# In sparse-attention branch B the parts of v become the stationary operand and the transposed probabilities of all tokens the moving one

## The chip, the cores and the metric

The program runs on one core of one Trainium2 chip. The metric is device microseconds for one execution of the whole program, which covers both layers; lower is better. The core has a matrix engine (TensorE, "PE" in the profile, with its weight loads listed apart as "PEld"), a vector engine (VectorE, "DVE"), a scalar engine (ScalarE, "ACT"), GpSimd ("POOL") and a sync engine that issues the DMAs ("SP").

## The reference

Two layers of a decoder trunk for 512 tokens of width 1024. Each layer projects the normed tokens, runs three token mixers A, B and C, multiplies each projected branch by a sigmoid gate, sums, projects out, and then runs a gated feed-forward network with a short convolution. Branch B is what the change touches: a small indexer has picked, for each query, its best causal keys, and four heads of 64 attend over these.

```python
def mixer_sparse(q, k, v, q_idx, k_idx, w_idx):
    ...
        att = jnp.einsum('bqhd,bqkhd->bhqk', qb, k_sel).astype(jnp.float32) * (HEAD_DIM ** -0.5)
        valid = idx <= qpos[None, :, None]
        att = jnp.where(valid[:, None], att, -jnp.inf)
        p = jax.nn.softmax(att, axis=-1).astype(v.dtype)
        return jnp.einsum('bhqk,bqkhd->bqhd', p, v_sel)
...
    y = (gates[:, :, 0] * (o_a @ w_br_a) + gates[:, :, 1] * (o_b @ w_br_b)
         + gates[:, :, 2] * (o_c @ w_br_c))
    return y @ w_out
```

In the kernel nothing is gathered: keys that were not picked get -1e30 from a mask, so a head's probabilities for a tile of 128 queries are a 128 x (128 (t+1)) block row, t = 0 to 3.

## The kernel before

**Numbers in two parts.** Matmul operands are in the type fp32r. To keep accuracy each operand is split into a high and a low part: `split` has ACT copy the high part (L81) and DVE subtract it from the source (L82). An ordinary product is then three matmuls (`mm3`, L88 to L90: high by high, high by low, low by high). A matmul here has a stationary operand of 128 x 128, loaded by an instruction of its own, and a moving operand of up to 512 columns.

**The order of the work.** `ORDER` lists, per layer, the projections of A, the indexer, C, B ("B", 0 and "B", 1, two heads each) and between and after them the gated branch projections ga, gc, gb. The last entries are B 0, B 1, gc (8 column blocks) and gb (8 column blocks). Attention is cut into chains of three steps S, T and V. `slot()`, called once after every projection tile and every column block of a branch, issues the T of one chain, the S of the next and the V of the one before, so that attention is woven into projections; functions given to `later` run some slots on. Before gb begins, slots are called until all chains are done (gb needs B's outputs `oTb`). The tile framework then orders each engine's instructions from a simulated timeline, so the order in the trace is not the program's to the letter: matmuls of a later block can be put among those of a chain.

**A chain of B** (`chains_b`). For a unit of two heads there are six chains: three groups of query tiles (`PARTS`: tiles 0 and 1; tile 2; tile 3) by two heads.
- S: score matmuls (L396, L397) into a PSUM bank `sc`; `masked_exp` adds the mask and takes the maximum on DVE (L470) and the exponential on ACT with the row's sum (L472), into `e`.
- T: `transpose_p` transposes the 128 x 128 blocks of `e` on PE (L477) into a bank `tp`, and splits it in one piece into `ph` and `pl` (L480, which are L81 and L82 on tiles `pt`). Per head there are 3 + 3 + 4 = 10 blocks.
- V: `pv_mm`, per block: the block of `ph` is stationary and v's high and low parts move (128 columns, L488), then the block of `pl` is stationary and v's high part moves (64 columns, L489). Outputs come with queries on partitions.

After two query tiles of both heads `PV.evac` adds the two column halves on DVE (L525). At the end DVE takes the reciprocal of the row sums (L648), multiplies the outputs by it (L650), and `to_oT` transposes four blocks on PE (L532) and splits them (L81, L82 on tiles `u`) into `oTb[i]`, which gb's matmuls (L88 to L90, `mm<-u`) read.

Branch C has chains of the same form, with two score rows each and a DVE step on their ratio (L675 to L680) before its transposes.

Of the kernel before, what the change touches and what calls it, by code (L numbers as in the profile page):

```python
# [9 lines left out]
F32 = mybir.dt.float32  # L10
F32R = mybir.dt.float32r
# [3 lines left out]
ALU = mybir.AluOpType  # L15
AX = mybir.AxisListType

P = 128
LO, HI = HALF = slice(0, 64), slice(64, 128)
S = 512  # L20
NT = S // P
# [3 lines left out]
HD = 64  # L25
# [24 lines left out]
def tile_trunk(ctx, tc, x, positions, w_in, w_br_a, w_br_b, w_br_c, w_out, lam_q1, lam_k1, lam_q2, lam_k2,  # L50
               subln_g, norm_mix_pre, norm_mix_post, norm_ffn_pre, norm_ffn_post,
               w_ffn_up, conv_w, conv_b, w_ffn_down, out):
    nc = tc.nc
# [7 lines left out]
    def alloc(shape, dtype, tag):  # L61
        uid[0] += 1
        return sb.tile(shape, dtype, tag=tag, name=f"{tag}{uid[0]}", bufs=SBUF_SLOTS[tag])

    def palloc(tag):
        uid[0] += 1
        return ps.tile([P, 512], F32, tag=tag, name=f"{tag}{uid[0]}",
                       bufs=PSUM_BANKS[tag])

    def small(n=8):  # L70
        return alloc([P, n], F32, "s")
# [7 lines left out]
    def split(hi, lo, src, scale=None):  # L79
        if scale is None:  # L80
            nc.scalar.copy(hi, src)  # L81
            nc.vector.tensor_tensor(lo, src, hi.bitcast(F32), op=ALU.subtract)  # L82
        else:
            nc.scalar.activation(hi, src, AF.Copy, scale=scale)
            nc.vector.scalar_tensor_tensor(lo, src, scale, hi.bitcast(F32), op0=ALU.mult, op1=ALU.subtract)
# [61 lines left out]
    for g in range(3):  # L147
        for p in range(2):
            b = 768 * g + p * P
            unit_cols["A", g, p] = [(b, P), (b + 256, P), (b + 512, P)]  # L150
    unit_cols["A", 0, 0] = unit_cols["A", 0, 0] + [(OFF_I + 512, 72)]
    for h in range(4):
        b = OFF_C + h * P
        unit_cols["C", h] = [(b, P), (b + 512, P), (b + 1024, P)]
    for p in range(2):
        b = OFF_B + p * P
# [57 lines left out]
    ident = cp.tile([P, P], F32, name="ident")  # L214
# [104 lines left out]
    chains = []  # L319
# [5 lines left out]
    def later(f, lag=1):  # L325
        pending.append([lag, f])
# [138 lines left out]
    def qk_mm(dst, qkT, h, q0, k0, n):  # L465
        ks = slice(k0, k0 + n)
        score_mm(dst, qkT[:, h, q0:q0 + P], qkT[:, 2 + 2 * h, ks], qkT[:, 3 + 2 * h, ks])

    def masked_exp(e, sc, mask, mneg, dcol):
        nc.vector.tensor_tensor_reduce(out=e, in0=sc, in1=mask, scale=-0.125, scalar=3e38,  # L470
                                       op0=ALU.add, op1=ALU.min, accum_out=mneg)
        nc.scalar.activation(e, e, AF.Exp, bias=mneg, scale=-1.0, accum_out=dcol)  # L472

    def transpose_p(e, nb):
        tp = palloc("tp")
        for b in range(nb):
            nc.tensor.transpose(tp[:, b * P:(b + 1) * P], e[:, b * P:(b + 1) * P], ident)  # L477
        ph = alloc([P, 512], F32R, "pt")
        pl = alloc([P, 512], F32R, "pt")
        split(ph[:, 0:nb * P], pl[:, 0:nb * P], tp[:, 0:nb * P])  # L480
        return ph, pl

    def pv_mm(dst, pT, blocks):

        nb = len(blocks)
        for i, (b, v) in enumerate(blocks):
            c = slice(b * P, (b + 1) * P)
            nc.tensor.matmul(dst, pT[0][:, c], v, start=i == 0, stop=False)  # L488
            nc.tensor.matmul(dst[:, 0, :], pT[1][:, c], v[:, 0, :], start=False, stop=i == nb - 1)  # L489


    PARTS = [[(0, 0), (1, P)], [(2, 0)], [(3, 0)]]

    class Chain:


        def __init__(self, S_, V_, fin=None):
            self.S_, self.V_, self.fin = S_, V_, fin

        def S(self):  # L500
            self.e, self.nb = self.S_()

        def T(self):
            self.pT = transpose_p(self.e, self.nb)

        def V(self):
            self.V_(self.pT)
# [20 lines left out]
    def to_oT(o, oTs, i, scale=None, lag=1):  # L528
        def go():
            tp = palloc("tp")  # L530
            for t in range(NT):
                nc.tensor.transpose(tp[:, t * P:(t + 1) * P], o[:, t, :], ident)  # L532
            oT = alloc([P, 2, S], F32R, "u")
            split(oT[:, 0, :], oT[:, 1, :], tp, scale=scale)
            oTs[i] = oT
        later(go, lag)
# [82 lines left out]
    def chains_b(qkT, v, masks, oTs, i):  # L619
        while score_jobs:  # L620
            score_jobs.pop(0)()
        while topk_steps:
            if next(topk_steps[0], None) is None:
                topk_steps.pop(0)
        pv = PV(2)
        dd = alloc([P, NT, 2], F32, "s")
        on = alloc([P, NT, P], F32, "th")
        for parts in PARTS:
            for h in range(2):
                def S_(parts=parts, h=h):  # L630
                    sc = palloc("sc")
                    e = alloc([P, 512], F32, "sm")
                    for t, c0 in parts:
                        qk_mm(sc[:, c0:c0 + (t + 1) * P], qkT, h, t * P, 0, (t + 1) * P)
                    for t, c0 in parts:
                        sl = slice(c0, c0 + (t + 1) * P)
                        mneg = small()
                        masked_exp(e[:, sl], sc[:, sl], masks[t], mneg[:, 0:1], dd[:, t, h:h + 1])
                    return e, sum(t + 1 for t, _ in parts)

                def V_(pT, parts=parts, h=h):
                    for t, c0 in parts:
                        pv_mm(pv.at(t, h), pT, [(c0 // P + b, v[:, b, h]) for b in range(t + 1)])
                        if t % 2 == 1 and h == 1:
                            pv.evac(t // 2, on[:, t - 1:t + 1, :])

                def fin():
                    nc.vector.reciprocal(dd, dd)  # L648
                    onv = on.rearrange("p t (h d) -> p t h d", h=2)
                    nc.vector.tensor_tensor(onv, onv, dd.unsqueeze(3).to_broadcast([P, NT, 2, HD]), op=ALU.mult)  # L650
                    to_oT(on, oTs, i)
                chains.append(Chain(S_, V_, fin if (parts, h) == (PARTS[-1], 1) else None))


    def chains_c(qkT, v, nlam, subg, oTs, i):
# [159 lines left out]
    for l in range(DEPTH):  # L815
# [21 lines left out]
        masks = [cmask[:, 384:512], wkB, wkA[:, 512:896], wkA[:, 0:512]]  # L837
# [3 lines left out]
        for u in ORDER:  # L841
# [20 lines left out]
            elif u[0] == "A":  # L862
                g, p = u[1], u[2]
# [7 lines left out]
                else:  # L871
                    def go(p=p, vq=vq):
                        def fin(opn):
                            on = combine_a(a1[p, 0]["o0"], a1[p, 0]["md"], opn)
                            to_oT(on, oTa, p, lag=4)
                        chains_a12(*a1[p, 1][::-1], *vq[::-1], a_scr[l][p], fin)
# [42 lines left out]
        for t in range(NT):  # L919
            acc = palloc(("sc", "mm", "mm", "mm")[t])  # L920
# [119 lines left out]
```

## Time and profile before

| | us |
|---|---|
| median of 3 runs | 1857.63 |
| lowest, highest | 1857.12, 1858.28 |
| the profiled execution, its own time | 1860.71 |
| its span from first to last instruction | 1858.9 |

The profile is of one execution. Busy times are per engine. A matmul's length in the trace is from its start to a modelled end, and neighbours overlap in it; the distance from one matmul's start to the next one's is what a matmul costs the engine. Starts are in us from the start of the span. A group's row has its instructions' count, busy us and mean ns, then the idle time of the engine just before them and what ended it.

### The profile page before, as it was taken

How to read it: one execution, taken by the hardware profiler on the slowest of the kernel's cores; microseconds unless marked ns; L12 is line 12 of the kernel's file. 1: busy time of each engine (PE TensorE's matmuls, PEld its weight loads, DVE VectorE, ACT ScalarE, POOL GpSimd, SP SyncE). 2: the span in 40 equal slices, each digit the busy share in tenths (PEclk: the TensorE clock that was granted, in tenths of full speed). 3: DMA queues.
4: the chain of work that ended last, by engine and by line, in shares of the span. 5: the costliest groups of instructions: out<-in, count | busy, mean ns of one | idle time of the engine just before them, and what ended most of it. 6: DMA issues, size and time to landing. Idle time of an engine off the chain costs nothing.

```text
span 1858.9 us, 25416 instructions
## 1 busy us (share of the span) xinstructions
PE 1834.1 (99%) x9565; PEld 1607.4 (86%) x9565; DVE 1155.1 (62%) x2138; ACT 867.7 (47%) x1518; POOL 28.3 (2%) x53
## 2 busy tenths in 40 slices
PE   8999999999999999999999999999999999999998
PEld 6999989988889888888889999789888798888886
DVE  6687798665457666642367787885545566666332
ACT  5665654463335444432256756545533354444221
POOL 0000000000000000000000000000000000000000
PEclk9999999999999999999999999999999999999999
DMA  5333323233343333333433333232332443332241
GB/s 162 90 80 101 85 66 84 70 91 90 104 143 121 105 102 91 96 100 126 127 105 84 80 99 89 78 79 77 97 98 86 149 123 98 103 94 91 102 152 64
DMA packets 265173, 185.22 MB, mean 100 GB/s; under 512 B 14710, under 2 KB 238298, under 8 KB 265050
## 3 DMA queue, kind: packets, MB, share of 16 engines
q1 hardware_dynamic: 265050, 183.60, 33.8%
q8 instruction: 75, 1.23, 0.3%
q14 instruction: 48, 0.39, 0.1%
HBM read 171.99 MB, written 11.57 MB: 99 GB/s over the span
## 4 chain that ended last, share of the span: by engine, by line
PE 67%; issue 20%; DVE 7%; DMA 3%; ACT 2%; SPq 1%; POOL 0%; DVEq 0%; POOLq 0%; ACTq 0%
PE mm L88 16%; PE mm L89 16%; PE mm L90 16%; PE sc L88 2%; PE sc L89 2%; PE sc L90 2%; PE pv L488 2%; PE sc L396 1%; PE sc L397 1%; PE tp L477 1%; DMA wr<-in_w_in_dram 1%; DVE wl L82 1%; PE pv L89 1%; PE pv L88 1%; PE pv L90 1%
## 5 line engine op out<-in xcount | busy, mean ns | idle before, releaser
L82 DVE TENSOR_TENSOR wl<-wr,wh 128x1024 fp32r<-128x1024 f32 (+2 forms) x314 | 359.1, 1146 | 369.5 <-ACT wh L81 368.6
L81 ACT CAST wh<-wr 128x1024 fp32r<-128x1024 f32 (+2 forms) x314 | 309.4, 989 | 458.0 <-PE mm L90 135.5
L88 PE MATMUL mm<-xh,wh 128*128 128x512 f32 (+1 forms) x784 | 297.6, 380 | 1.3 <-ACT xh L81 0.8
L89 PE MATMUL mm<-xl,wh 128*128 128x512 f32 (+1 forms) x784 | 297.3, 379 | 0.0
L90 PE MATMUL mm<-xh,wl 128*128 128x512 f32 (+1 forms) x784 | 297.2, 379 | 0.0
L89 PE MATMUL mm<-wl,xh 128*128 128x384 f32 (+2 forms) x816 | 283.0, 348 | 0.9 <-DVE wl L82 0.9
L90 PE MATMUL mm<-wh,xl 128*128 128x384 f32 (+2 forms) x816 | 283.6, 348 | 0.0
L88 PE MATMUL mm<-wh,xh 128*128 128x384 f32 (+2 forms) x816 | 281.5, 348 | 1.3 <-ACT xh L81 0.7
L88 PEld LDWEIGHTS mm<-xh,wh 128*128 128x128 f32 x784 | 147.9, 189 | 27.8 <-ACT xh L81 1.2
L89 PEld LDWEIGHTS mm<-xl,wh 128*128 128x128 f32 x784 | 147.7, 188 | 26.2 <-DVE xl L82 0.4
L90 PEld LDWEIGHTS mm<-xh,wl 128*128 128x128 f32 x784 | 147.8, 188 | 26.1
L89 PEld LDWEIGHTS mm<-wl,xh 128*128 128x128 f32 x816 | 154.4, 189 | 5.7 <-DVE wl L82 1.9
L88 PEld LDWEIGHTS mm<-wh,xh 128*128 128x128 f32 x816 | 154.4, 189 | 5.7 <-ACT xh L81 1.7
L90 PEld LDWEIGHTS mm<-wh,xl 128*128 128x128 f32 x816 | 154.4, 189 | 4.0 <-DVE s L226 0.3
L90 PE MATMUL sc<-xh,wl 128*128 128x512 f32 (+1 forms) x272 | 99.2, 365 | 0.0
L89 PE MATMUL sc<-xl,wh 128*128 128x512 f32 (+1 forms) x272 | 99.0, 364 | 0.0
L88 PE MATMUL sc<-xh,wh 128*128 128x512 f32 (+1 forms) x272 | 98.8, 364 | 0.0
L88 PE MATMUL mm<-wh,qk 128*128 128x512 f32 x216 | 85.8, 397 | 0.0
L89 PE MATMUL mm<-wl,qk 128*128 128x512 f32 x216 | 85.4, 396 | 0.0
L90 PE MATMUL mm<-wh,qk 128*128 128x512 f32 x216 | 85.1, 396 | 0.0
L488 PE MATMUL pv<-v,pt 128*128 128x128 f32 (+1 forms) x280 | 71.2, 297 | 2.7 <-ACT pt L81 2.7
L472 ACT ACTIVATE sm<-sm,s 128x128 f32<-128x128 f32 (+2 forms) x96 | 53.5, 558 | 43.3 <-DVE s L470 43.1
(274 smaller groups left out, 3251.8 us busy)
## 6 DMA issues: line engine op xcount, KB each, us to landing
wr<-in_w_ffn_up_dram SPq DMA_DIRECT2D x176, 256.0 KB, 3.4
wr<-in_w_in_dram SPq DMA_DIRECT2D x282, 128.0 KB, 2.5
wr<-in_w_in_dram SPq DMA_DIRECT2D x56, 512.0 KB, 3.9
wr<-in_w_ffn_down_dram SPq DMA_DIRECT2D x44, 512.0 KB, 3.7
wr<-in_w_out_dram SPq DMA_DIRECT2D x16, 512.0 KB, 3.6
xd<-u SPq DMA_DIRECT2D x12, 512.0 KB, 3.7
u<-xd SPq DMA_DIRECT2D x12, 512.0 KB, 5.2
u<-in_x_dram SPq DMA_DIRECT2D x8, 512.0 KB, 5.9
```

Source lines behind the costliest of these rows:

```text
L81: nc.scalar.copy(hi, src)
L82: nc.vector.tensor_tensor(lo, src, hi.bitcast(F32), op=ALU.subtract)
L88: nc.tensor.matmul(dst, a[0], b[0], start=start, stop=False)
L89: nc.tensor.matmul(dst, a[0], b[1], start=False, stop=False)
L90: nc.tensor.matmul(dst, a[1], b[0], start=False, stop=stop)
L396: nc.tensor.matmul(dst, q, kh, start=True, stop=False)
L397: nc.tensor.matmul(dst, q, kl, start=False, stop=True)
L472: nc.scalar.activation(e, e, AF.Exp, bias=mneg, scale=-1.0, accum_out=dcol)
L477: nc.tensor.transpose(tp[:, b * P:(b + 1) * P], e[:, b * P:(b + 1) * P], ident)
L488: nc.tensor.matmul(dst, pT[0][:, c], v, start=i == 0, stop=False)
```

## The change

In `chains_b` the operands of the last product change places. v's high and low parts side by side (128 columns of one key block and head) are stationary, and the transposed probabilities move, for all query tiles that can see this key block at once: 512, 384, 256 and 128 columns for key blocks 0 to 3. High and low parts of the probabilities are moved one after the other, so a head has 8 matmuls into one bank `acc`. Its rows 0 to 63 are the part from v's high half and rows 64 to 127 that from v's low half; ACT copies the lower one out and DVE adds them. The output then has its dimension on partitions and tokens along the columns, as `oTb` needs it.

For this the transposed blocks of all of a head's chains are kept in one tile `g` (a buffer of the kind `qk`), and are split into it by query tile, and tile 3's fourth block apart: five splits for a head where there were three. The matmuls of a head all stand in V of its last chain. Chains run head by head instead of group by group. As queries are now columns, the rows' sums can't be applied at the end, so each S takes their reciprocal and scales `e`. The end of a unit is a split of `of` without transposes.

```diff
--- before.py
+++ after.py
@@ -494,14 +494,14 @@
     class Chain:
 
 
-        def __init__(self, S_, V_, fin=None):
-            self.S_, self.V_, self.fin = S_, V_, fin
+        def __init__(self, S_, V_, fin=None, T_=None):
+            self.S_, self.V_, self.fin, self.T_ = S_, V_, fin, T_ or transpose_p
 
         def S(self):
             self.e, self.nb = self.S_()
 
         def T(self):
-            self.pT = transpose_p(self.e, self.nb)
+            self.pT = self.T_(self.e, self.nb)
 
         def V(self):
             self.V_(self.pT)
@@ -622,11 +622,11 @@
         while topk_steps:
             if next(topk_steps[0], None) is None:
                 topk_steps.pop(0)
-        pv = PV(2)
-        dd = alloc([P, NT, 2], F32, "s")
-        on = alloc([P, NT, P], F32, "th")
-        for parts in PARTS:
-            for h in range(2):
+        dd = alloc([P, 2, NT, 2], F32, "md")
+        of = alloc([P, S], F32, "th")
+        for h in range(2):
+            hold = []
+            for parts in PARTS:
                 def S_(parts=parts, h=h):
                     sc = palloc("sc")
                     e = alloc([P, 512], F32, "sm")
@@ -635,21 +635,51 @@
                     for t, c0 in parts:
                         sl = slice(c0, c0 + (t + 1) * P)
                         mneg = small()
-                        masked_exp(e[:, sl], sc[:, sl], masks[t], mneg[:, 0:1], dd[:, t, h:h + 1])
+                        masked_exp(e[:, sl], sc[:, sl], masks[t], mneg[:, 0:1], dd[:, 0, t, h:h + 1])
+                    t0, t1 = parts[0][0], parts[-1][0] + 1
+                    nc.vector.reciprocal(dd[:, 1, t0:t1, h], dd[:, 0, t0:t1, h])
+                    for t, c0 in parts:
+                        sl = slice(c0, c0 + (t + 1) * P)
+                        nc.vector.tensor_scalar(e[:, sl], e[:, sl], dd[:, 1, t, h:h + 1], None, op0=ALU.mult)
                     return e, sum(t + 1 for t, _ in parts)
 
-                def V_(pT, parts=parts, h=h):
+                def T_(e, nb, parts=parts, hold=hold):
+
+
+                    if not hold:
+                        hold.append(alloc([P, 6, S], F32R, "qk"))
+                    g = hold[0]
+                    tp = palloc("tp")
+                    for b in range(nb):
+                        nc.tensor.transpose(tp[:, b * P:(b + 1) * P], e[:, b * P:(b + 1) * P], ident)
                     for t, c0 in parts:
-                        pv_mm(pv.at(t, h), pT, [(c0 // P + b, v[:, b, h]) for b in range(t + 1)])
-                        if t % 2 == 1 and h == 1:
-                            pv.evac(t // 2, on[:, t - 1:t + 1, :])
+                        n = min(t + 1, 3)
+                        ts = slice(t * P, (t + 1) * P)
+                        split(g[:, 0:n, ts], g[:, 3:3 + n, ts], tp[:, c0:c0 + n * P].rearrange("p (b c) -> p b c", b=n))
+                        if t == 3:
+                            split(g[:, 1, 0:P], g[:, 4, 0:P], tp[:, 384:512])
+                    return g
+
+                def V_(g, parts=parts, h=h):
+                    if parts is not PARTS[-1]:
+                        return
+                    acc = palloc("pv")
+                    for b in range(NT):
+                        row, cols = (b, slice(b * P, S)) if b < 3 else (1, slice(0, P))
+                        for w in range(2):
+                            nc.tensor.matmul(acc[:, b * P:S], v[:, b, h].rearrange("p s d -> p (s d)"),
+                                             g[:, 3 * w + row, cols], start=b + w == 0, stop=b == 3 and w == 1)
+                    low = alloc([P, S], F32, "pt")
+                    nc.scalar.copy(low[LO], acc[HI])
+                    nc.vector.tensor_tensor(of[HALF[h]], acc[LO], low[LO], op=ALU.add)
 
                 def fin():
-                    nc.vector.reciprocal(dd, dd)
-                    onv = on.rearrange("p t (h d) -> p t h d", h=2)
-                    nc.vector.tensor_tensor(onv, onv, dd.unsqueeze(3).to_broadcast([P, NT, 2, HD]), op=ALU.mult)
-                    to_oT(on, oTs, i)
-                chains.append(Chain(S_, V_, fin if (parts, h) == (PARTS[-1], 1) else None))
+                    def go():
+                        oT = alloc([P, 2, S], F32R, "u")
+                        split(oT[:, 0, :], oT[:, 1, :], of)
+                        oTs[i] = oT
+                    later(go)
+                chains.append(Chain(S_, V_, fin if (parts, h) == (PARTS[-1], 1) else None, T_))
 
 
     def chains_c(qkT, v, nlam, subg, oTs, i):
```

## Rows read from the trace of the kernel before

**Rows 1.** The page's parts on the whole span: busy time of the engines, and the clock granted to PE in 40 slices of the span (9 is 90% or more of full speed).
```profile
PE 1834.1 (99%) x9565; PEld 1607.4 (86%) x9565; DVE 1155.1 (62%) x2138; ACT 867.7 (47%) x1518; POOL 28.3 (2%) x53
...
PEclk9999999999999999999999999999999999999999
```

**Rows 2.** The chain of work that ended last, by engine, as shares of the span ("issue" is time in which nothing that the profile shows was waited for).
```profile
PE 67%; issue 20%; DVE 7%; DMA 3%; ACT 2%; SPq 1%; POOL 0%; DVEq 0%; POOLq 0%; ACTq 0%
```

**Rows 3.** Busy time by stretch, one stretch among B's chains in each layer: length, then busy us (and instructions) of PE, PEld, DVE, ACT and POOL, PE's granted clock, share of the DMA engines, GB/s.
```profile
435.00:455.00 20.00, 20.00 (x102) 16.94 (x101) 8.75 (x14) 6.51 (x11) 0.00 (x0) 1.00 0.30 79
...
1360.00:1380.00 20.00, 20.00 (x103) 16.94 (x102) 9.79 (x17) 7.46 (x14) 0.00 (x0) 1.00 0.30 82
```

**Rows 4.** Groups on PE from 383 to 478 us, the stretch of layer 0 in which B's chains run: the two matmuls of a block, and the transposes of the outputs.
```profile
L488 PE MATMUL pv<-v,pt 128*128 128x128 f32 x40 | 9.5, 283 | 0.0
L489 PE MATMUL pv<-v,pt 128*128 128x64 f32 x40 | 9.0, 240 | 0.0
...
L532 PE MATMUL tp<-ident,th 128*128 128x128 f32 x8 | 1.2, 272 | 0.0
```

**Rows 5.** PE in order of time, the first and the last of eight matmuls of one chain of B that stand together, L489 and L488 by turns, and the two 512-column matmuls behind them (start, length, engine, line).
```profile
1391.21 0.19 PE L489 MATMUL pv<-v,pt 128*128 128x64 f32 x1
...
1391.91 0.31 PE L488 MATMUL pv<-v,pt 128*128 128x128 f32 x1
1392.06 0.45 PE L88 MATMUL mm<-xh,wh 128*128 128x512 f32 x1
1392.34 0.40 PE L89 MATMUL mm<-xl,wh 128*128 128x512 f32 x1
```

**Rows 6.** PE in order of time, unbroken streams of one width: the first and the last of eight matmuls of 512 columns, of four of 384, of four of 256. Then, from the page's groups, the matmuls of one line of `mm3` and the weight loads of that line.
```profile
300.77 0.34 PE L90 MATMUL mm<-wh,xl 128*128 128x384 f32 x1
...
301.29 0.34 PE L90 MATMUL mm<-wh,xl 128*128 128x384 f32 x1
...
568.03 0.28 PE L90 MATMUL mm<-xh,wl 128*128 128x256 f32 x1
...
568.38 0.28 PE L90 MATMUL mm<-xh,wl 128*128 128x256 f32 x1
...
1400.09 0.39 PE L88 MATMUL mm<-xh,wh 128*128 128x512 f32 x1
...
1401.68 0.39 PE L89 MATMUL mm<-xl,wh 128*128 128x512 f32 x1
...
L89 PE MATMUL mm<-wl,xh 128*128 128x384 f32 (+2 forms) x816 | 283.0, 348 | 0.9 <-DVE wl L82 0.9
...
L89 PEld LDWEIGHTS mm<-wl,xh 128*128 128x128 f32 x816 | 154.4, 189 | 5.7 <-DVE wl L82 1.9
```

**Rows 7.** PE in order of time at the four output transposes of unit 0 of layer 0, merged into one row, and what follows.
```profile
438.86 0.60 PE L532 MATMUL tp<-ident,th 128*128 128x128 f32 x4
439.29 0.49 PE L477 MATMUL tp<-ident,sm 128*128 128x128 f32 x3
```

**Rows 8.** Groups on DVE and on ACT from 383 to 478 us that answer to operations which the change removes or adds, and one row in order of time, a tensor-by-constant operation on DVE.
```profile
L82 DVE TENSOR_TENSOR pt<-tp,pt 128x384 fp32r<-128x384 f32 x8 | 4.4, 553 | 0.5 <-ACT pt L81 0.5
L82 DVE TENSOR_TENSOR pt<-tp,pt 128x512 fp32r<-128x512 f32 x4 | 2.8, 689 | 2.9 <-ACT pt L81 2.9
L525 DVE TENSOR_REDUCE th<-pv 128x256 f32<-128x512 f32 x4 | 2.8, 688 | 4.5 <-PE pv L489 4.4
...
L650 DVE TENSOR_TENSOR th<-th,s 128x512 f32<-128x512 f32 x2 | 1.4, 692 | 0.1
L391 DVE TENSOR_TENSOR qk<-tp,qk 64x512 fp32r<-64x512 f32 x2 | 1.4, 684 | 0.6 <-ACT qk L390 0.6
...
L81 ACT CAST pt<-tp 128x384 fp32r<-128x384 f32 x8 | 3.8, 476 | 6.0 <-PE tp L477 6.0
...
L390 ACT CAST qk<-tp 64x512 fp32r<-64x512 f32 x4 | 2.3, 582 | 0.4 <-PE tp L425 0.4
...
344.25 0.42 DVE L748 TENSOR_SCALAR u<-u 128x512 f32<-128x512 f32 x1
```

**Rows 9.** All engines in order of time at the end of B in layer 1, from the last chain's transposes to the first matmul that reads unit 1's outputs (an idle time just before an instruction, and what ended it, stands in brackets).
```profile
1387.19 0.60 PE L477 MATMUL tp<-ident,sm 128*128 128x128 f32 x4
...
1393.66 0.24 PE L489 MATMUL pv<-v,pt 128*128 128x64 f32 x1
...
1397.24 0.50 PE L88 MATMUL mm<-xh,wh 128*128 128x512 f32 x1 [0.27 <-ACT th L762]
...
1397.87 0.68 DVE L82 TENSOR_TENSOR u<-tp,u 128x512 fp32r<-128x512 f32 x1
...
1401.90 0.61 PE L88 MATMUL mm<-u,wh 128*128 128x512 f32 x2
```

**Rows 10.** Busy time by stretch (columns as in rows 3) where slots run without a projection beside them, in branch C just ahead of ga, in layer 0 and in layer 1.
```profile
261.00:265.00 4.00, 2.16 (x14) 1.37 (x12) 4.00 (x10) 2.67 (x7) 0.00 (x0) 1.00 0.33 73
265.00:269.00 4.00, 3.66 (x16) 3.21 (x15) 4.00 (x11) 1.83 (x4) 0.00 (x0) 0.57 0.10 26
...
1177.00:1184.00 7.00, 4.05 (x20) 2.53 (x18) 7.00 (x19) 4.07 (x9) 0.80 (x1) 0.94 0.21 53
1184.00:1191.00 7.00, 7.00 (x25) 5.96 (x25) 6.92 (x16) 3.16 (x7) 0.00 (x0) 0.57 0.02 6
```

**Rows 11.** DVE in order of time in an S of branch C: the reciprocal of a row sum, and what it waited for.
```profile
342.14 0.17 DVE L675 RECIPROCAL s<-s 128x2 f32<-128x2 f32 x1 [0.99 <-ACT sm L472]
```

## Prediction, made before the change was run

> **What bounds the kernel now.** I read the page's sum of busy times first: PE is busy for 1834.1 of 1858.9 us, DVE for 62% and ACT for 47%, and the clock was at full speed in every slice [rows 1]. The reader should distrust the 99%, since neighbouring matmuls overlap in the records; so the chain of waits comes second: PE holds 67% of it, and most of the rest is "issue", in which nothing was waited for, while DMA has 3% and DVE 7% [rows 2]. The busy times by stretch among B's chains come third, because a mean over the span says nothing about the stage that changes. In both layers PE is busy there for 20.00 of 20 us, at a clock of 1.00, while DVE works 8.75 to 9.79 us, ACT 6.51 to 7.46, and the DMA engines 0.30 of the time [rows 3]. So in this stage PE sets the pace, and every microsecond that one of its instructions costs is a microsecond of the kernel. The last question is what an instruction costs on PE, and that is read from the distances between starts, not from lengths.
>
> **PE, the product with v.** In the stretch of layer 0 there are 40 blocks, each with a matmul of 128 columns and one of 64 [rows 4]: four heads with ten blocks, 20 matmuls a head, 8 heads in two layers. Eight of them stand together from 1391.21 to the 512-column matmul at 1392.06, whose own successor is at 1392.34 [rows 5]. An unbroken stream of 512 columns steps by (1401.68 - 1400.09) / 7 = 0.227 us [rows 6]. I take one such step off the 1.13 us: 0.90 us for eight, 0.113 us each, although four of them move 128 columns and four 64. At the 512-column pace of 0.44 ns a column those would be 0.057 and 0.028 us. The columns do not set this price; what each instruction has in common is a load of 128 x 128 of its own, as every matmul here has (816 matmuls and 816 loads of one line, rows 6). A head costs 20 x 0.113 = 2.26 us.
>
> After the change a head has two matmuls each of 512, 384, 256 and 128 columns. Streams give 0.227 us, 0.52 / 3 = 0.173 us and 0.35 / 3 = 0.117 us for the first three [rows 6]: the loads are inside these steps. For 128 columns I take 0.113. Sum: 2 x (0.227 + 0.173 + 0.117 + 0.113) = 1.26 us. A head saves 1.00 us, eight heads 8.0 us. Bounds: if no load were hidden, each of the eight would cost 0.113 us more and a head would save 0.10, all of them 0.8 us; if a 128-column matmul cost its columns alone, 0.057, a head would save 1.11 us, all of them 8.9. I take 8.0, as the streams in rows 6 are of the same form.
>
> **PE, the output transposes.** Eight in layer 0's stretch [rows 4], 16 in the kernel. Four take 439.29 - 438.86 = 0.43 us [rows 7], so 16 cost 1.7 us, all gone. The ten transposes of probabilities and the scores of each head stay. PE's sum: -8.0 - 1.7 = -9.7 us.
>
> A rule speaks against the first term. The Trainium skill, "TensorE: Matmul & The Clock Gate", section "Back-to-back issue gap", gives an isolated step of columns / 2.4 + 2.5 ns; an estimate by it is 0.85 us a head before and 1.09 us after, so 1.9 us lost over eight heads, and 0.9 us won on the transposes. Its section "LDWEIGHTS (loading the stationary operand)" gives columns / 1.2, an estimate of 0.107 us for 128, and the trace agrees with that one: 0.113 us whatever the columns.
>
> **DVE and ACT.** Per head DVE gets three reciprocals at 0.17 [rows 11], the scaling of 128 + 256 + 384 + 512 columns (0.42 us for 512 in the nearest row, a tensor by a constant, so 1.05 by columns; at the other end 0.69 for 512 as for the two-tensor operations, 1.7), and a final add of 64 x 512 at 0.684 [rows 8]. Its splits go from 2 x 0.553 + 0.689 to 2 x 0.553 and one of 256 and two of 128 columns; on the line through 0.553 and 0.689 those are 0.42 and 0.28, so 0.29 us more. It loses the evacuation (0.688 a head) and its share of the multiply (0.692 a unit, 0.35 a head). Net +1.5 to +2.2 us a head, 6 to 9 us per layer. ACT gets the copy of 64 x 512 at 0.582 and some 0.3 us of extra splits: +0.9 us a head, under 4 us per layer. The work that hides it is the projection and gate matmuls that PE does for some 95 us per layer: DVE has over 10 us idle in each 20, ACT over 12 [rows 3]. Priced at nothing; if that cover were gone it would be at most 9 + 4 us per layer.
>
> **Waits.** Each S now has DVE wait for ACT's row sum before its reciprocal; in branch C, which does this already, DVE sat 0.99 us [rows 11]. Behind it on DVE stand the low parts of the weights and the splits of other chains, and PE waits for the weights. There are 24 such S. PE showed no idle time among B's chains, and DVE's idle half covers it: nothing.
>
> All eight matmuls of a head now wait for the last split of its last chain, where earlier ones could start before. That matters once per layer, at the end of B, where gb needs unit 1's outputs. Before, the last transposes start at 1387.19, the last product ends at about 1393.7, the outputs are split by 1397.87 + 0.68 = 1398.55, and the first matmul that reads them starts at 1401.90 [rows 9]: 3.35 us of slack, filled with gate matmuls of the next block. After, S is longer by about 1.0 + 0.17 + 0.42 us, T by a small split, while behind the product come a copy of 0.58, an add of 0.68, and a split of about 0.58 + 0.69: 2.5 us where it was 4.8. The two balance, the slack stays, and I price it at nothing. No DMA is added, removed or moved. The four extra `qk` buffers per layer come round to ones whose readers are finished.
>
> **The sum.** 1860.7 us for the profiled execution (span 1858.9 and 1.8 around it) - 9.7 = 1851.0. The median is 3.1 us below that execution, so 1857.6 - 9.7 = 1847.9; I say 1848. A measurement of this kernel can tell about 0.2%, 3.7 us, from no change.
>
> **The rivals.**
> - Columns set the pace (the rule above, as a mechanism of this kernel). At 0.444 ns a column, a head goes from 1920 columns, 0.85 us, to 2560, 1.14: +2.3 us in all, and 16 transposes of 0.057 give back 0.9: +1.4, 1859 us. Rows 5 speak against it: 64 and 128 columns would not cost the same. 3%.
> - PE stalls at the end of B. Where slots run without cover, ahead of ga, PE did 2.16 of 4 us and then ran at a mean clock of 0.57, so partly at 1.2 of 2.4 GHz, for 4 us: 1.8 + 0.3 + 1.7 = 3.9 us lost; in layer 1 it was 2.95 + 0.4 + 3.0 = 6.4 us [rows 10]. Once per layer that takes back 3.9 to 12.8 us: between 1852 and 1861. It decides if the outputs come more than 3.35 us later than now [rows 9]. 10%.
> - DVE's waits reach PE, the case on the slower side. With none of 24 waits of 0.99 us covered, +23.8 - 9.7 = +14.1: 1872 us. The place is the S step; it ends slower once more than (9.7 + 3.7) / 0.99, 14 of 24, are exposed. DVE's idle half speaks against it, branch C's stalls [rows 10] for it. 7%.
> - Something else feeds the stage (weights, order of the instructions), so that PE's saved time comes back as idle: 1856 to 1858 us. Rows 3 speak against it, with DMA at 0.30. 5%.
>
> **How the numbers follow.** The forecast, PE's time saved and nothing lost, has 75%, and spans 1845 to 1851: 8.9 + 1.7 us saved at best, 3 us of small stalls at worst, and a slow-clock stretch as in rows 10 that lengthens or shortens in either layer. The range to 1855 takes in the milder half of the stall at the end of B. Faster holds the forecast and part of that stall, 0.80; same the rest of it, the columns and the feed, 0.13; slower DVE's waits, 0.07.
>
> **What would show it.** Right: 64 matmuls in place of 160 with steps of about 0.227, 0.173, 0.117 and 0.113 us; no transposes behind the product; both stretches of B shorter by some 4.8 us; PE still without idle time there; DVE busier by 6 to 9 us per layer. Wrong: steps of the new matmuls longer by a load; PE waiting at the start of gb for tile `u`, or for `wl` behind a reciprocal; a new stretch with a granted clock under 1.

## The result

The changed kernel took 1849.24 us in the median where the kernel before took 1857.83 beside it: 0.995 of its time, 95% interval 0.9939 to 0.996. In a second series it took 1846.83 against 1856.82, 0.9948 [0.9934, 0.9961]. The forecast was 1848, by 9.7 us less; measured were 8.6 and 10.0 us less, and 9.9 in a third series, which stands below under the tries ahead of ga.

The page's part on busy times and the engines' shares of the chain that ended last, of the changed kernel (answering to [rows 1, 2]):

```profile
PE 1822.6 (99%) x9453; PEld 1596.3 (86%) x9453; DVE 1166.2 (63%) x2202; ACT 874.8 (47%) x1542; POOL 28.1 (2%) x53
...
PE 78%; issue 11%; DVE 6%; DMA 3%; ACT 1%; SPq 1%; POOL 0%; DVEq 0%; POOLq 0%; ACTq 0%
```

PE has 112 matmuls fewer: 96 of the product (160 became 64) and 16 transposes. Its busy time is down 11.5 us, DVE's up 11.1 and ACT's up 7.1. Busy time by stretch among B's chains (as [rows 3]), and the new matmuls as groups on PE from 378 to 478 us (as [rows 4]):

```profile
435.00:455.00 20.00, 20.00 (x96) 16.59 (x95) 11.69 (x23) 8.36 (x18) 0.00 (x0) 1.00 0.30 80
1360.00:1380.00 20.00, 20.00 (x100) 16.76 (x99) 12.24 (x29) 9.22 (x20) 0.00 (x0) 1.00 0.28 80
```

```profile
L670 PE MATMUL pv<-qk,v 128*128 128x512 f32 x8 | 2.7, 403 | 0.0
L670 PE MATMUL pv<-qk,v 128*128 128x384 f32 x8 | 2.0, 337 | 0.0
L670 PE MATMUL pv<-qk,v 128*128 128x256 f32 x8 | 1.6, 283 | 0.0
L670 PE MATMUL pv<-qk,v 128*128 128x128 f32 x8 | 1.3, 249 | 0.0
```

PE is still busy for all of the 20 us, at a granted clock of 1.00, with DVE at 12 us instead of 9 to 10. What a product costs now is seen in order of time, at the last head of layer 1 (PE alone; eight matmuls of falling width are merged into one row):

```profile
1385.19 1.37 PE L670 MATMUL pv<-qk,v 128*128 128x512 f32 x8
1386.40 0.45 PE L88 MATMUL mm<-xh,wh 128*128 128x512 f32 x1
1386.69 0.40 PE L89 MATMUL mm<-xl,wh 128*128 128x512 f32 x1
```

Read as [rows 5]: 1386.69 - 1385.19 = 1.50, less one step of 0.227, is 1.27 us for a head.

**A measure that is steadier than the whole time.** From series to series the median of the kernel before moved by up to 1.4 us and that of the changed kernel by up to 2.4, although nothing was changed. For one stage there is a better measure: the time from the first masked maximum on tile `m` in a layer, which only B uses, to the first matmul of the output projection. It holds B's chains and the blocks of gc and gb. The two rows of layer 0 and the two of layer 1, first of the kernel before, then of the changed one:

```profile
385.55 0.42 DVE L470 CUSTOM_DVE_ANT_0 sm<-sc,m 128x256 f32<-128x256 f32 x1
519.44 0.39 PE L88 MATMUL mm<-wh,qk 128*128 128x512 f32 x1
1305.86 0.42 DVE L470 CUSTOM_DVE_ANT_0 sm<-sc,m 128x256 f32<-128x256 f32 x1
1439.70 0.39 PE L88 MATMUL mm<-wh,qk 128*128 128x512 f32 x1
```

```profile
385.91 0.42 DVE L470 CUSTOM_DVE_ANT_0 sm<-sc,m 128x256 f32<-128x256 f32 x1
514.25 0.39 PE L88 MATMUL mm<-wh,qk 128*128 128x512 f32 x1
1300.57 0.42 DVE L470 CUSTOM_DVE_ANT_0 sm<-sc,m 128x256 f32<-128x256 f32 x1
1429.11 0.39 PE L88 MATMUL mm<-wh,qk 128*128 128x512 f32 x1
```

133.89 and 133.84 us became 128.34 and 128.54. The two layers agree within 0.2 us, and the gain of the two, 10.85 us, is near that of the profiled executions, 10.53 (1860.71 to 1850.18). The 0.2 us come from the first of the two instructions, which is on DVE. Taken from a matmul a little ahead of B's chains (L88 `mm<-u`, at 378.46 us before and 378.63 after, the same one in PE's order) and its like in layer 1, the stage is 140.98 and 140.97 us before and 135.62 in both layers after, again 135.62 in both layers of the second series: 5.36 us less per layer, 10.7 in all, with 56 matmuls fewer in each. The first measure, read for every kernel that ran and bears on the change (each layer, the difference of both together to the kernel before, and beside it the difference of the medians in the same series):

| kernel | stage, layer 0 + layer 1, us | to before | median to before |
|---|---|---|---|
| before | 133.89 + 133.84 | | |
| changed | 128.34 + 128.54 | -10.9 | -8.6 |
| changed, second series | 128.54 + 128.54 | -10.7 | -10.0 |
| changed, third series | 128.42 + 128.54 | -10.8 | -9.9 |
| product in pieces of 128 | 133.10 + 133.19 | -1.4 | -1.3 |
| before, wider low part | 133.92 + 133.96 | +0.2 | -0.3 |
| 64 transposes put back | 131.78 + 131.79 | -4.2 | -4.1 |
| no scaling | 128.64 + 128.63 | -10.5 | -10.5 |
| three more DVE passes | 131.29 + 131.31 | -5.1 | -3.3 |
| unit 0 alone, first series | 131.27 + 131.35 | -5.1 | -2.9 |
| unit 1 alone, first series | 131.21 + 131.19 | -5.3 | -3.2 |
| unit 0 alone, second series | 131.33 + 131.34 | -5.1 | -2.1 |
| unit 1 alone, second series | 131.22 + 131.21 | -5.3 | -3.1 |

### The profile page after: what moved, and what is told of

Same layout as the page of the kernel before. It is cut to its first block, busy times and chain, and to the rows that moved or that the text cites. A ratio compares the mean times of both kernels' runs of the same rounds, so it can differ in the third digit from the quotient of the medians.

```text
span 1848.4 us, 25255 instructions
## 1 busy us (share of the span) xinstructions
PE 1822.6 (99%) x9453; PEld 1596.3 (86%) x9453; DVE 1166.2 (63%) x2202; ACT 874.8 (47%) x1542; POOL 28.1 (2%) x53
## 4 chain that ended last, share of the span: by engine, by line
PE 78%; issue 11%; DVE 6%; DMA 3%; ACT 1%; SPq 1%; POOL 0%; DVEq 0%; POOLq 0%; ACTq 0%
PE mm L88 17%; PE mm L89 17%; PE mm L90 17%; PE sc L89 4%; PE sc L90 4%; PE sc L88 4%; PE pv L89 2%; PE pv L90 2%; PE pv L88 2%; PE sc L396 1%; PE sc L397 1%; PE pv L488 1%; DVE wl L82 1%; DMA wr<-in_w_in_dram 1%; PE tp L477 1%
## 5 line engine op out<-in xcount | busy, mean ns | idle before, releaser
L88 PE MATMUL mm<-xh,wh 128*128 128x512 f32 (+1 forms) x784 | 296.9, 379 | 0.8 <-ACT xh L81 0.8
L88 PE MATMUL mm<-wh,xh 128*128 128x384 f32 (+2 forms) x816 | 281.0, 348 | 1.2 <-ACT wh L81 0.8
L88 PEld LDWEIGHTS mm<-xh,wh 128*128 128x128 f32 x784 | 147.9, 189 | 27.1 <-ACT xh L81 1.3
L88 PEld LDWEIGHTS mm<-wh,xh 128*128 128x128 f32 x816 | 154.2, 189 | 5.4 <-ACT xh L81 1.1
L88 PE MATMUL sc<-xh,wh 128*128 128x512 f32 (+1 forms) x272 | 98.8, 364 | 0.0
L88 PE MATMUL mm<-wh,qk 128*128 128x512 f32 x216 | 85.8, 397 | 0.0
L412 ACT COPY qr<-mm 128x384 f32<-128x384 f32 x96 | 45.6, 478 | 56.2 <-PE mm L90 55.5
```

Source lines behind the costliest of these rows:

```text
L88: nc.tensor.matmul(dst, a[0], b[0], start=start, stop=False)
L412: nc.scalar.copy(qr[:, t], acc[:, 0:384])
```

## The experiments

The theory: PE sets the pace in this stage, and a small matmul costs PE the load of its stationary operand, 0.113 us, whether it moves 64 columns or 128. The rivals: columns set the pace; the gain lies at the end of a unit; DVE's added work reaches PE. "The stage" is the time between the two instructions of the table.

### The product in pieces of 128 columns

```diff
                         for w in range(2):
-                            nc.tensor.matmul(acc[:, b * P:S], v[:, b, h].rearrange("p s d -> p (s d)"),
-                                             g[:, 3 * w + row, cols], start=b + w == 0, stop=b == 3 and w == 1)
+                            for t in range(b, NT):
+                                c = slice(cols.start + (t - b) * P, cols.start + (t - b + 1) * P)
+                                nc.tensor.matmul(acc[:, t * P:(t + 1) * P], v[:, b, h].rearrange("p s d -> p (s d)"),
+                                                 g[:, 3 * w + row, c], start=b + w + t == 0, stop=b == 3 and w == 1)
```

> The changed kernel, but each of the new matmuls is cut into pieces of 128 columns with the same stationary operand: 20 instructions a head instead of 8, the same 2560 columns. Theory that a small matmul costs its weight load (0.113 us whatever the columns): a head goes from 1.27 back to 20 x 0.113 = 2.26 us, eight heads +7.9 us, so 1849.2 + 7.9 = 1857 us, with steps of 0.11 us between the pieces. Rival, columns set the pace: no change, 1849 us, with steps of 0.057 us. Rival, the gain was in the output transposes and the order of the work and not in the product: 1849 us as well, with any step.

Measured: 1856.97 us in the median, 0.9992 [0.9983, 1.0001] of the kernel before. PE in order of time, 17 pieces merged into one row, and the next matmul:

```profile
409.68 2.01 PE L672 MATMUL pv<-qk,v 128*128 128x128 f32 x17
411.52 0.52 PE L654 MATMUL tp<-ident,sm 128*128 128x128 f32 x3
```

(411.52 - 409.68) / 17 = 0.108 us a piece, twice what 128 columns cost at the pace of the wide streams. The same columns in 20 instructions a head instead of 8 give the gain back, all but 1.4 us in the stage; the 16 transposes, 1.7 us, are gone here too. Of the 9.3 us that the two layers' stage got longer, 7.1 are the product (eight heads at 20 x 0.108 instead of 1.27 us), and 0.9 have no term. The rest are PE's waits for ACT at a gate's tile `th`, which rose to 1.7 us from 0.4 in the changed kernel (the list of waits, PE alone; us in total, times, longest):

```profile
PE mm L88 <- ACT th L794: 1.7, 2, 0.8
```

Both rivals that expected no change fall. This is the theory's strongest test, since neither the order of the chains in the program nor DVE's work (1166.6 us busy, 1166.2 in the changed kernel) differs from the changed kernel.

### The kernel before with 64 columns more in 200 instructions

```diff
+            if v.shape[-1] == HD:
+                nc.tensor.matmul(dst, pT[1][:, c], v, start=False, stop=i == nb - 1)
+            else:
                 nc.tensor.matmul(dst[:, 0, :], pT[1][:, c], v[:, 0, :], start=False, stop=i == nb - 1)
```

> The kernel before, but where a head is 64 wide (branches A and B) the matmul of the low part of the probabilities moves v's high and low half, 128 columns instead of 64. This adds 64 columns to 200 instructions and no instruction. Theory that the load sets the price: the pair steps by 0.226 us as before, 1857.8 us, within 1 us. Rival, columns set the pace: 200 x 64 x 0.444 ns = +5.7 us, 1863.5 us.

Measured: 1857.95 us, 0.9999 [0.999, 1.0008]; the stage is 0.2 us longer. Eight matmuls of one chain, the first and the last, and what follows, as in [rows 5] but all of 128 columns:

```profile
1388.74 0.22 PE L490 MATMUL pv<-v,pt 128*128 128x128 f32 x1
...
1389.47 0.28 PE L488 MATMUL pv<-v,pt 128*128 128x128 f32 x1
1389.58 0.44 PE L88 MATMUL mm<-xh,wh 128*128 128x512 f32 x1
1389.87 0.40 PE L89 MATMUL mm<-xl,wh 128*128 128x512 f32 x1
```

1389.87 - 1388.74 - 0.227 = 0.90 us for the eight, as before with half of them at 64 columns. The 64 extra columns were free. This settles the rival "columns". An estimate by the Trainium skill's "TensorE: Matmul & The Clock Gate", section "LDWEIGHTS (loading the stationary operand)", is 0.107 us for a load of 128 columns, and the trace agrees, with 0.108 and 0.113 us measured. The isolated step by columns in the section "Back-to-back issue gap" of the Trainium skill's "TensorE: Matmul & The Clock Gate" is not what a small matmul costs in this stage.

Neither run parts the load from some other fixed price of an instruction, because every matmul here has one load, and no kernel with fewer columns in the stationary operand was run. The trace of the kernel before speaks for the load (loads, PEld, and matmuls, PE, in order of time, inside [rows 5]):

```profile
1391.33 0.19 PEld L489 LDWEIGHTS pv<-v,pt 128*128 128x128 f32 x1
1391.38 0.24 PE L489 MATMUL pv<-v,pt 128*128 128x64 f32 x1
1391.44 0.19 PEld L488 LDWEIGHTS pv<-v,pt 128*128 128x128 f32 x1
1391.46 0.30 PE L488 MATMUL pv<-v,pt 128*128 128x128 f32 x1
1391.55 0.19 PEld L489 LDWEIGHTS pv<-v,pt 128*128 128x128 f32 x1
1391.61 0.24 PE L489 MATMUL pv<-v,pt 128*128 128x64 f32 x1
```

The loads start 0.11 us apart each time, while the matmuls, of 64 and 128 columns by turns, start 0.08 and 0.15 us apart. The even beat is that of the loads.

### The output transposes put back four times over

```diff
                     def go():
+                        for _ in range(4):
+                            tp = palloc("tp")
+                            for t in range(NT):
+                                nc.tensor.transpose(tp[:, t * P:(t + 1) * P], of[:, t * P:(t + 1) * P], ident)
                         oT = alloc([P, 2, S], F32R, "u")
```

> The changed kernel with 16 transposes of 128 x 128 put back at the end of each unit, four times what stood there before, their results unread; 64 in the kernel. Theory that PE sets the pace and a transpose costs 0.108 us: +6.9 us, 1856 us, which makes the 16 that the change removed worth 1.7 us. Rival, the transposes were hidden in waits at the end of a unit: under 2 us more, 1849 to 1851 us. Rival, they delay gb's first read and let PE stall: more than 10 us.

Nothing reads what the 64 transposes write. Measured: 1854.19 us, 0.998 [0.9971, 0.9989], which is 5 us over the changed kernel's first median; the stage of both layers is 6.6 us longer than the mean of the changed kernel's first two series. Eight of the transposes and the two matmuls behind them:

```profile
438.29 1.03 PE L681 MATMUL tp<-ident,th 128*128 128x128 f32 x8
439.08 0.48 PE L90 MATMUL mm<-xh,wl 128*128 128x512 f32 x1
439.39 0.39 PE L88 MATMUL mm<-xh,wh 128*128 128x512 f32 x1
```

(439.39 - 438.29 - 0.227) / 8 = 0.109 us, so 64 cost PE 7.0 us and the stage shows 6.6; the 0.4 us that PE waits at `th` in the changed kernel's stage are not there in this one. The term of 1.7 us for the 16 that were removed stands. They were neither hidden nor worth more through a wait.

### Without the scaling

```diff
-                    t0, t1 = parts[0][0], parts[-1][0] + 1
-                    nc.vector.reciprocal(dd[:, 1, t0:t1, h], dd[:, 0, t0:t1, h])
-                    for t, c0 in parts:
-                        sl = slice(c0, c0 + (t + 1) * P)
-                        nc.vector.tensor_scalar(e[:, sl], e[:, sl], dd[:, 1, t, h:h + 1], None, op0=ALU.mult)
```

> The changed kernel without the reciprocals and the scaling of the probabilities by them: the part left out is the softmax's division in branch B. Theory that PE sets the pace and DVE's added work is hidden: 1849 us, within 1 us. Rival, DVE's wait for ACT's row sum holds PE up: up to 1 us less (the distance of the forecast to the measured time), 1848 us; if it holds more, the time falls by more.

Measured: 1847.75 us, 0.9947 [0.9935, 0.996], the changed kernel's own ratio; the stage is 128.64 and 128.63 us, no shorter than with the scaling, although DVE is busy for 12.4 us less (1153.8 instead of 1166.2). The reciprocals, their waits and the scaling cost nothing.

### Three more passes on DVE

```diff
                         nc.vector.tensor_scalar(e[:, sl], e[:, sl], dd[:, 1, t, h:h + 1], None, op0=ALU.mult)
+                        for _ in range(3):
+                            nc.vector.tensor_scalar(e[:, sl], e[:, sl], 1.0, None, op0=ALU.mult)
```

> The changed kernel with three more passes over every scaled tile on DVE, each a multiplication by 1.0: 96 instructions and at 0.42 us for 512 columns some 25 us of DVE time more, all in the stretches of branch B and each in a chain's path. Theory that DVE's idle half beside the projections covers it: 1849 us, within 1 us. Rival, DVE's added work reaches PE (through the splits of the weights that stand behind it, or through a later end of B): each 3 us of extra DVE time that is not covered shows as such, up to +25 us, 1874 us; a quarter of it would be 1855 us.

Measured: 1854.21 us, 0.9982 [0.9973, 0.999]; the stage is 2.9 us longer per layer than in the changed kernel, and DVE is busy for 23.0 us more in all. So the cover has an end, and not everywhere the same. The stretch where it ends in layer 0, first in the changed kernel, then here (columns as in [rows 3]), and PE in order of time there:

```profile
412.00:421.00 9.00, 9.00 (x49) 7.76 (x49) 7.16 (x19) 6.17 (x14) 0.00 (x0) 1.00 0.22 58
```

```profile
407.00:412.00 5.00, 5.00 (x23) 4.13 (x22) 4.74 (x11) 3.79 (x8) 0.00 (x0) 1.00 0.24 72
412.00:421.00 9.00, 7.34 (x43) 5.78 (x43) 8.07 (x30) 7.16 (x18) 0.00 (x0) 1.00 0.23 59
421.00:426.00 5.00, 5.00 (x23) 4.13 (x23) 5.00 (x15) 2.37 (x8) 0.00 (x0) 1.00 0.01 3
```

```profile
414.53 0.50 PE L672 MATMUL pv<-qk,v 128*128 128x512 f32 x1 [0.52 <-ACT qk L81]
415.32 0.50 PE L396 MATMUL sc<-qk 128*128 128x512 f32 x1 [0.29 <-DVE s L470]
...
417.77 0.33 PE L672 MATMUL pv<-qk,v 128*128 128x128 f32 x1 [0.35 <-DVE qk L82]
...
419.44 0.44 PE L396 MATMUL sc<-qk 128*128 128x384 f32 x1 [0.49 <-DVE s L470]
```

From 412 to 421 us unit 0's last chains and unit 1's first stand together. In this kernel hardly a projection or gate matmul is among them before 419.9 us, in the changed one there are many, so the order differs beside DVE's work; DVE is already at 7.16 of 9 us in the changed kernel. There, and at the same place in layer 1, PE waits for the splits into `qk` and for the maxima behind them. The four waits shown are 1.65 us of idle time, less than the 2.9 us that the stage got longer. The rest fits an estimate: at each wait the overlap of neighbours is lost as well, some 0.16 us behind the matmul that stands before it (a record of 512 columns is 0.39 us long where its step is 0.227) and some 0.1 us in the one after it (0.50 instead of 0.39), so 1.0 us for four. Both theories were partly wrong: not all of the cover holds, and what fails is one place per layer of 9 us, not a share of all DVE work. The changed kernel itself stays on the safe side of it, with PE at 9.00 of 9.

### One unit alone

Both forms of `chains_b` stand in these kernels, and the planner picks by unit:

```diff
-                later(lambda vq=vq, p=u[1]: chains_b(vq[1], vq[0], masks, oTb, p), 3)
+                later(lambda vq=vq, p=u[1]: (chains_b_old if p == 1 else chains_b)(vq[1], vq[0], masks, oTb, p), 3)
```

> The new form in unit 0 of branch B alone, the old one in unit 1, in both layers. Unit 0 ends beside the projections of gc, unit 1 at the wait ahead of gb. Theory that PE sets the pace all along: half of the gain, 4.0 + 0.9 = 4.9 us by the sum, so 1857.8 - 4.9 = 1853 us. Rival, the end of B in front of gb is where it is lost or won: the whole gain or none, 1849 or 1858 us.

> The new form in unit 1 of branch B alone, the old one in unit 0, in both layers. Theory that PE sets the pace all along: the other half of the gain, 1853 us, the same as with unit 0 alone. Rival, the later product of a head costs something ahead of gb: less gain than unit 0 alone has, by the stall; if the shorter path behind the product helps there, more.

Measured: 1854.58 us, 0.9989 [0.998, 0.9999], for unit 0 alone (2.9 us less than before), and 1854.31, 0.9984 [0.9975, 0.9993], for unit 1 alone (3.2 less). Neither is the whole gain or none, but 6.1 is short of 8.6. They ran once more beside the whole change:

> The changed kernel once more, beside the two half changes, so that all three stand against the same executions of the kernel before. Theory that the two units' gains add: the difference to before is the sum of the two halves' differences within 1.5 us, and 9.7 us by the sum of the parts (8.6 measured first). Rival, the halves disturb each other or the whole helps itself: a whole that differs from the sum by 3 us or more, as the first measurements would have it (8.6 against 2.9 and 3.2).

> The new form in unit 0 alone, again, beside the whole change. Theory: 4.9 us less than before by the sum, 4.3 by half of what the whole measured first. Rival, as measured first: 2.9 us less.

> The new form in unit 1 alone, again, beside the whole change. Theory: 4.9 us less than before by the sum, 4.3 by half of what the whole measured first. Rival, as measured first: 3.2 us less.

Measured: 1846.83 for the whole (10.0 less than before), 1854.73 for unit 0 alone (2.1 less, 0.9987 [0.9978, 0.9996]) and 1853.76 for unit 1 alone (3.1 less, 0.9984 [0.9975, 0.9993]). By the medians the halves do not add: 5.2 us together against 10.0 for the whole, as the rival has it. By the stage they do: 5.1 + 5.3 = 10.4 against 10.7 us for the whole, so in the place that was changed the units are worth the same and are independent, and the end of B in front of gb is no special place. What the medians of the halves lack against the stage, 2 to 3 us each, is not in it. Nor is it behind the last stage, where every profiled execution of the table takes 419.2 to 419.4 us to its end; it must lie ahead of the two stages. There two executions of one kernel differ by 2 us and more (below). A part belongs to the kernel: just ahead of ga in layer 1, PE waits at the transposes of branch A's outputs (L532) for 0.46 us before, for 1.43 and 1.10 in the first two series of the changed kernel, for 0.38 and 0.46 with unit 0 alone, and for 1.50 and 1.53 with unit 1 alone. What else there is stays open.

### Two tries on the stalls ahead of ga

```diff
-                    slot()
+                    slot(0)
```

`slot(0)` adds nothing to the count of selection steps that a slot issues.

> The changed kernel, but the slots that are called without a projection beside them issue no step of the key selection on DVE; those steps move to the later slots. The stretches ahead of ga show DVE busy throughout (7.00 of 7 us) and PE idle, and then a clock of 0.60 to 0.81. Theory that DVE's selection steps stand in the way of the chains that PE waits for there: PE's idle time and the slow clock behind it shrink, up to 10 us less, some 1841 to 1846 us. Rival, the chain of one head itself (maximum, exponential, row sum, transposes, split) is too long for slots without cover: no change, 1849 us. Rival, the steps come too late and hold up branch B: more than 1851 us.

Measured: 1847.58 us, 0.995 [0.9937, 0.9962], the changed kernel's ratio. The stretch ahead of ga in layer 1:

```profile
1170.00:1177.00 7.00, 3.66 (x19) 2.14 (x18) 7.00 (x19) 3.76 (x9) 0.76 (x1) 1.00 0.22 54
```

DVE is busy for all of the 7 us, with selection steps (L775) still among its work. In the trace PE's 9453 matmuls, DVE's 2202 instructions and ACT's 1542 stand in the same order as in the changed kernel, one by one, by operation, tiles and shapes. So the edit changed nothing that ran, and it tells nothing about the cause of that stall. The run counts as a third series of the changed kernel, 9.9 us below the kernel before.

```diff
-        ("C", 2), ("ga", 0, 4), ("C", 3), ("ga", 4, 8), ("B", 0)
+        ("C", 2), ("C", 3), ("ga", 0, 4), ("ga", 4, 8), ("B", 0)
```

> The changed kernel with the projection of C's last head put ahead of the first half of ga instead of behind it, so that the slots which wait for branch A's outputs there become fewer. Theory that PE's idle time and slow clock ahead of ga come from slots without a projection: up to 10 us less, 1839 to 1846 us. Rival, the stall moves to where C's last chains then stand: no change, 1849 us, or slower if more chains stand there without cover.

Measured: 1867.04 us, 1.0056 [1.0044, 1.0069]. The forecast gain did not come. The stall became longer, and the granted clock stayed down for longer, in layer 1:

```profile
1205.00:1213.00 8.00, 4.00 (x20) 2.91 (x19) 6.88 (x21) 3.15 (x11) 1.04 (x1) 0.62 0.25 67
1213.00:1221.00 8.00, 7.69 (x21) 5.87 (x22) 8.00 (x24) 4.16 (x12) 0.00 (x0) 0.52 0.00 0
```

In layer 0 PE is idle for 9.5 of the 60 us from 280 to 340 us, 3.5 of them in a second stall, from 320 on, where the changed kernel's PE is busy throughout. That more chains of C now stand in the gap, as one rival has it, is likely but was not shown. No version tried is clearly faster than the changed kernel.

## Why the prediction was right

- **PE bounds the stage.** Right: what PE saved by the sum, 9.7 us, is near what the stage (10.7 to 10.9) and the medians (8.6, 10.0 and 9.9) show. About 1 us of the stage's gain has no term in the sum; 0.2 of it are shorter waits at `th` (0.27 us per layer before, 0.18 after), the rest stays unexplained. That two medians come within 0.3 us of the forecast is partly luck: the stage gained more, and what lies ahead of it moves a median by 1 to 2 us.
- **The product, 2.26 to 1.26 us a head.** 1.27 us measured after; the price per load was tested from both sides, with more instructions at equal columns and more columns at equal instructions.
- **The transposes, 1.7 us.** 0.109 us each where 0.108 was taken.
- **DVE and ACT, priced at nothing.** Right for the change: without the scaling the stage is no shorter. The forecast of 12 to 18 us for DVE was high, 11.1 came; ACT's 7.1 met the forecast of 0.9 a head. But the reason given, an idle half on the mean over 20 us, was too coarse: in the changed kernel there is one stretch per layer in which DVE has only 2 of 9 us left, and the extra passes used it up.
- **The waits for the row sum.** 0.99 us each was the price if exposed [rows 11]. DVE in fact sat far less, 1.2 us over 12 reciprocals of a layer (groups on DVE from 378 to 478 us):

```profile
L640 DVE RECIPROCAL md<-md 128x1 f32<-128x1 f32 x8 | 1.2, 155 | 1.0 <-ACT sm L472 1.0
L640 DVE RECIPROCAL md<-md 128x2 f32<-128x2 f32 x4 | 0.6, 161 | 0.2 <-ACT sm L472 0.2
```

- **The end of B.** The slack was to stay at 3.35 us. In layer 1 the outputs are split by 1388.59 + 0.69 = 1389.28, 2.9 us behind the product's end instead of 4.8, and the first reader starts at 1391.91, 2.6 us later; no wait for tile `u` is listed:

```profile
1387.22 0.68 DVE L674 TENSOR_TENSOR th<-pv,pt 64x512 f32<-64x512 f32 x1 [0.43 <-ACT pt L673]
1388.59 0.69 DVE L82 TENSOR_TENSOR u<-th,u 128x512 fp32r<-128x512 f32 x1 [0.69 <-ACT u L81]
...
1391.91 0.61 PE L88 MATMUL mm<-u,wh 128*128 128x512 f32 x2
```

- **The rivals.** Columns: shown wrong. DVE's waits: not there in the change, but real with 23 us more of DVE work. The feed: PE waited for 0.2 us per layer in the stage. The stall in front of gb: did not come. Its price was mis-added: "once per layer" at 3.9 us would be 7.8 at least, not 3.9.
- **A reading that was too coarse.** "The clock was at full speed in every slice" holds for slices of some 46 us, in which a 9 stands for 90% or more; [rows 10] show 0.57 inside such slices, ahead of ga and outside the stage.

## What to carry to other kernels

Where PE is busy throughout, price a matmul by the distance between starts in a stream of its own width. Ask first whether a fixed price per matmul (here most likely the load of the stationary operand) or the moved columns set it. At 64 and 128 columns the fixed price did, 0.108 to 0.113 us; at 256 the two were about even, with a step of 0.117. In such a case let that operand move which makes the moves wide and few, even if more columns move in all: here 2560 columns a head in 8 matmuls cost 1.27 us and 1920 in 20 cost 2.26. Test such a price from both sides, with more instructions and with more columns. And for a change worth half a per cent, measure the stage between two fixed instructions beside the whole time: here it repeated within 0.2 us, and within 0.02 us with both instructions on PE, where medians moved by 2.

## What had not been expected of the hardware

The slow clock behind the stalls ahead of ga lasted differently long in two executions of one kernel, on two chips. Unit 0 alone, layer 1, the stall and the stretch behind it, first series and second series:

```profile
1168.00:1179.00 11.00, 8.64 (x40) 6.30 (x38) 10.22 (x32) 7.45 (x20) 1.02 (x1) 1.00 0.35 85
1179.00:1187.00 8.00, 7.39 (x31) 6.40 (x32) 7.92 (x19) 2.96 (x7) 0.00 (x0) 0.79 0.11 31
```

```profile
1168.00:1179.00 11.00, 9.47 (x44) 7.20 (x44) 10.18 (x30) 6.64 (x19) 1.02 (x1) 1.00 0.33 86
1179.00:1187.00 8.00, 6.33 (x21) 5.35 (x22) 7.98 (x21) 4.28 (x10) 0.00 (x0) 0.57 0.19 49
```

At a mean clock of 0.79 and 0.57 over 8 us, between the two levels of 2.4 and 1.2 GHz, up to 1.7 and 3.4 us were lost, after PE had been busy for 8.64 and 9.47 of the 11 us ahead of it. PE ran the same matmuls in the same order there both times, and the time from the end of layer 0's stage to the start of layer 1's was 1.6 us longer in the second series (784.81 and 786.43 us). This alone is as large as the term of the transposes, and it lies outside the stage that was changed.
